# Two 1024-cubed projections of a transformer block as seven block products each, with their weight-side operands formed earlier

## The chip, the cores and the metric

The kernel runs on one core of a Trainium2 chip. It is hand-written for the engines: TensorE (PE) multiplies, VectorE (DVE), ScalarE (ACT) and GpSimd (POOL) do the elementwise work, and SyncE (SP) issues almost all transfers between HBM and the on-chip memory SBUF. The metric is the device time of one execution in microseconds (us); lower is better. Before the change it is 1440.81 us, the median of three executions (1439.41 to 1441.95).

## The reference

One layer of a mixer block on 1024 latent tokens and 256 context tokens of width 1024. A combined input projection feeds a convolution branch and an attention branch of 16 query heads on 4 key/value heads; two learned gates merge the branches, one output projection follows, and a normalised, gated residual ends the layer. Cut to what matters here:

```python
def merge_branches(y_conv, y_attn, gm, w_out):
    ga, gb = jnp.split(gm, 2, axis=-1)
    return (jax.nn.sigmoid(ga) * y_conv + jax.nn.sigmoid(gb) * y_attn) @ w_out
...
        o = latent_attention(q, k_all, v_all)
        y_attn = (o * jax.nn.silu(gate_b)) @ w_attn_out[l]
        y_conv = conv_module(ua, gate_a, conv_w[l], conv_b[l], ln_g[l], ln_b[l], w_conv_out[l])
        out = merge_branches(y_conv, y_attn, gm, w_out[l])
        x_new = x + gt[:, None, :] * rms_norm(out, g_post[l])
```

The change concerns the two products `@ w_attn_out` and `@ w_out`, each 1024 tokens by 1024 by 1024. `gt` is the third part of `silu(c) @ w_mod + b_mod`.

## The kernel before, in words

All products are carried out on float32 values that are split into a high part (a cast to the PE's reduced format) and a low part (the rest): `split` (L106) casts on ACT and subtracts on DVE or POOL, and `mm3` (L116) is one product of three matmuls, high by high, low by high and high by low. A "k step" below is one such group of three on 128 rows of the contraction and 512 columns. A 1024-cubed product has 8 x 2 output tiles of 128 x 512 and 8 k steps in each, that is 16 x 24 = 384 matmuls.

The program has stages. After the modulation and the normalisation comes the phase of **queries, keys and values** (L1171 to L1203): a loop over 4 key/value groups and 4 quarters of the tokens, 16 pieces in all. In each piece the PE computes one piece of q, k and v (24 x 2 matmuls into the PSUM tiles po, the values and keys and queries by tokens), transposes the one before, and works off `per` = 21 steps of `filler`. `filler(1)` takes one k step from a long stream of other projections (`proj`, L141: gates, convolution inputs), so that the PE always has something to do. `pump` interleaves the taps of the depthwise convolution on DVE. The attention stage (to L1305) interleaves score matmuls, softmax and value matmuls with the rest of the same stream, the last of which is the convolution's output projection. For each of 16 pairs (a head pair and a half of the tokens) `pair_end` (L862) divides the attention output O by its row sums, splits it in high and low and stores both to HBM (ogD).

The **tail** starts at L1309. `og_load` (L1038) reads the 32 halves of ogD (256 KB each) into `ogs` between the last filler steps. `attn_out_job` (L1046) is the attention projection: 8 output rows j x 2 halves hf x 24 matmuls; each output tile is gated and added to the convolution branch on DVE (from tgbD and mcD, the stored gate and gated convolution output), then split again for the next product. Beside it `wparts` loads and splits w_attn_out, and `wout_load` (L1072) loads and splits w_out. At (3, 1) of this loop `post_gate` (L1012) computes the vector gt: 8 loads of 512 KB of w_mod, two matmuls for each, a small round trip through HBM, and GP = the broadcast gate times the norm's weight. `w_out` (L1084) then runs over 8 rows of 128 tokens: 48 matmuls, ACT squares and sums, DVE scales, POOL takes the power for the norm, DVE adds the residual x, SP stores.

What sets the order: PE, DVE, ACT and POOL are wrapped (class `Ordered`, L41). While an engine is "held" it runs in the order of the program text; DVE, ACT and POOL are held up to the end of the q/k/v phase (L1215), the PE up to L1312. Where an engine isn't held, and on SP's queue everywhere, a scheduler places the instructions at build time. Every engine, SP too, runs its own list strictly in order: an instruction that waits stops all behind it. SP's transfers are assigned in turn to eight semaphores, and a transfer also waits for the one eight before it ("DMAHW0" to "DMAHW7" below). A tile name with n buffers (`tl(tag, shape, n)`) makes the n-th next tile of this name wait until the first has been read.

## Time and profile before

| | us |
|---|---|
| three executions, median (range) | 1440.81 (1439.41 to 1441.95) |
| the profiled execution, its own time | 1438.2 |
| its span in the trace (rows are counted from the span's start) | 1436.4 |
| PE busy | 1384.3 (96%) |
| DVE / ACT / POOL busy | 999.4 / 550.5 / 533.7 |
| first matmul of the attention projection | 1238.23 |
| first matmul of the output projection | 1342.85 |
| end of the last matmul | 1430.17 |

The profile gives, for one execution, the busy time of each engine (section 1), the span in 40 slices (section 2), the chain of work that ended last, followed back from the end (section 4), and groups of equal instructions (section 5). The chain is also printed in order of time: start, duration, engine and tile, and the number of instructions. Most lines carry L51, the line of the recording wrapper, so tiles and not lines tell the places apart: ppj, ps, pm and po are the PSUM tiles, ogs the loaded attention output, whi and wlo the split weights. A view of windows gives each engine's busy time in a stretch, with the DMA share and GB/s behind it.

### The profile page before, as it was taken

What the parts mean: (1) busy time and instruction counts of PE and PEld (TensorE: products, weight loads), DVE (VectorE), ACT (ScalarE), POOL (GpSimd) and SP (SyncE); (2) the same over time, 40 slices, a digit from 0 to 9 for tenths busy, and PEclk for the clock granted to TensorE, in tenths of its full rate; (3) what the DMA queues carried; (4) which work ended last, traced back from release to release, by engine and by line L of the source; (5) the groups of instructions that cost most, each with busy time, mean ns of one, the idle gap of its engine ahead of it and who ended that gap; (6) DMA issues with size and microseconds to landing.
All of it is one profiled execution on the core that took longest, in us unless ns stands there. A gap on an engine that the chain in (4) does not pass through costs nothing.

```text
span 1436.4 us, 18677 instructions
## 1 busy us (share of the span) xinstructions
PE 1384.3 (96%) x6584; PEld 1051.2 (73%) x6584; DVE 999.4 (70%) x1289; ACT 550.5 (38%) x1358; POOL 533.7 (37%) x359
## 2 busy tenths in 40 slices
PE   5988999999999999989999999999999999999998
PEld 3776889888888977756666766666766666676886
DVE  4478779888788898997688577777686643263532
ACT  5532334343443431334445454444543342031211
POOL 2124324233242220355577565666455553000000
PEclk9999999999999999999999999999999999999999
DMA  9513323224222329213355244644364223967522
GB/s 337 198 52 119 98 67 124 78 89 134 89 69 78 101 75 256 90 47 123 104 188 189 102 145 155 196 146 145 113 189 142 93 75 110 321 210 221 178 88 73
DMA packets 115898, 194.12 MB, mean 135 GB/s; under 512 B 16558, under 2 KB 46806, under 8 KB 115804
## 3 DMA queue, kind: packets, MB, share of 16 engines
q1 hardware_dynamic: 106076, 176.08, 37.6%
q10 hardware_dynamic: 9728, 16.85, 4.1%
q8 instruction: 52, 0.85, 0.2%
q14 instruction: 42, 0.34, 0.1%
HBM read 134.20 MB, written 58.55 MB: 134 GB/s over the span
## 4 chain that ended last, share of the span: by engine, by line
PE 78%; DVE 9%; DMA 5%; issue 3%; ACT 2%; POOL 2%; SPq 1%; ACTq 0%; DVEq 0%; POOLq 0%
PE ppj L51 33%; PE po L51 22%; PE ps L51 12%; PE pm L51 11%; DVE acc L51 3%; DMA ogs<-ogD 2%; DVE mx L51 1%; DVE y L51 1%; DMA wraw<-in_wch 1%; DVE ts L51 1%; DVE wlo L51 1%; DVE pconv L51 1%; DMA r<-r1D 1%; DMA wm<-in_wmod 1%; POOL wlo L51 0%
## 5 line engine op out<-in xcount | busy, mean ns | idle before, releaser
L51 PE MATMUL ppj<-t,whi 128*128 128x512 f32 x1728 | 611.9, 398 | 5.0 <-DVE t L51 2.6
L51 PEld LDWEIGHTS ppj<-t,whi 128*128 128x128 f32 x1728 | 326.5, 189 | 90.3 <-issue 17.7
L51 PE MATMUL ppj<-t,wlo 128*128 128x512 f32 x864 | 339.1, 392 | 3.1 <-POOL wlo L51 3.1
L51 DVE TENSOR_REDUCE mx<-pm 128x1 f32<-128x512 f32 (+1 forms) x320 | 213.5, 682 | 93.6 <-PE pm L51 91.0
L51 ACT ACTIVATE pe<-ps 128x512 f32<-128x512 f32 x320 | 190.2, 598 | 194.1 <-PE ps L51 166.4
L51 DVE SCALAR_TENSOR_TENSOR pconv<-y,cw,pconv 128x1020 f32<-128x1020 f32 (+14 forms) x157 | 200.8, 1279 | 7.4 <-ACT pconv L51 3.6
L51 POOL TENSOR_TENSOR psum<-psum,pe 128x512 f32<-128x512 f32 x128 | 190.2, 1503 | 36.6 <-ACT pe L51 32.5
L51 PE MATMUL ps<-r,kk 128*128 128x512 f32 (+1 forms) x640 | 200.8, 395 | 3.1 <-ACT pe L51 3.1
L51 PEld LDWEIGHTS ppj<-t,wlo 128*128 128x128 f32 x864 | 163.4, 189 | 33.0 <-POOL wlo L51 3.4
L51 PE MATMUL po<-pe,vt 128*64 128x512 f32 x640 | 144.4, 597 | 0.0
L51 PEld LDWEIGHTS ps<-r,kk 128*128 128x128 f32 (+1 forms) x640 | 119.6, 188 | 33.2 <-ACT pe L51 6.5
L51 PE MATMUL pm<-kk,r 128*128 128x512 f32 (+1 forms) x384 | 128.3, 363 | 8.3 <-DVE mx L51 8.0
L51 POOL TENSOR_TENSOR psum<-psum,part 128x512 f32<-128x512 f32 x64 | 88.1, 1379 | 124.7 <-DVE part L51 120.2
L51 PE MATMUL po<-wgh,t 128*128 128x384 f32 x512 | 133.4, 342 | 0.0
L51 POOL TENSOR_TENSOR wlo<-wraw,whi 128x512 fp32r<-128x512 f32 x57 | 79.9, 1414 | 119.4 <-ACT whi L51 96.1
L51 DVE SCALAR_TENSOR_TENSOR acc<-y,cw,acc 128x1017 f32<-128x1017 f32 (+14 forms) x77 | 114.5, 1499 | 0.7
L51 ACT CAST whi<-wraw 128x512 fp32r<-128x512 f32 x126 | 77.3, 630 | 76.0 <-PE ppj L51 45.0
L51 PEld LDWEIGHTS po<-pe,vt 128*64 128x64 f32 x640 | 43.1, 136 | 84.8 <-issue 84.8
L51 PEld LDWEIGHTS po<-wgh,t 128*128 128x128 f32 x512 | 95.6, 193 | 1.3
L51 PEld LDWEIGHTS pm<-kk,r 128*128 128x128 f32 x384 | 73.3, 191 | 27.5 <-DVE mx L51 10.8
L51 DVE TENSOR_TENSOR wlo<-wraw,whi 128x512 fp32r<-128x512 f32 x69 | 59.4, 862 | 46.0 <-ACT whi L51 39.9
L51 PE MATMUL po<-wgl,t 128*128 128x384 f32 x256 | 87.7, 342 | 3.0 <-POOL wgl L51 3.0
(209 smaller groups left out, 1581.5 us busy)
## 6 DMA issues: line engine op xcount, KB each, us to landing
wraw<-in_wch SPq DMA_DIRECT2D x96, 256.0 KB
wm<-in_wmod SPq DMA_DIRECT2D x16, 512.0 KB
r1D<-r1st SPq DMA_DIRECT2D x32, 256.0 KB
y<-accD SPq DMA_DIRECT2D x16, 512.0 KB
r<-r1D ACTq DMA_DIRECT2D x32, 256.0 KB
ogD<-og SPq DMA_DIRECT2D x32, 256.0 KB
ogs<-ogD SPq DMA_DIRECT2D x32, 256.0 KB
x<-in_x SPq DMA_DIRECT2D x8, 512.0 KB
```

The source lines that it names most:

```text
L51: i = f(*a, **k)
```

## The change

Both projections of the tail are computed as seven products of half-size blocks. Each operand is cut into 2 x 2 blocks of 512 x 512 (block number b = 2 x row half + column half); sums and differences of blocks (the tables LEFT, RIGHT and DATA) are multiplied in the order of `STEPS`, and the results are added up to the four output blocks. One of the 14 `block_step`s is 4 output tiles t x 4 k steps x 3 matmuls = 48 matmuls; 14 x 48 = 672 stand for 2 x 384 = 768.

The weight-side operands depend on weights alone. `operands()` makes them in the q/k/v phase: 16 batches (side 0 for w_attn_out, side 1 for w_out; 4 t; 2 halves u), each with 4 loads of 128 KB (`blk`, 4 buffers), then seven operands, of which four need a sum or difference on POOL; each operand is split (cast on ACT, difference on POOL, `opw`, 2 buffers) and stored to HBM (opD, 256 KB a time, 112 stores). The counter `rest` advances it: one operand per two filler steps, from the second piece on; `run(ops)` does what is left at the phase's end. The rope tables move to the same `blk` buffers.

The data-side operands are formed in the tail: `heads_load` reads the attention output (now stored once, unsplit, by `pair_end`) as 16 tiles O4; `data_split` forms sums on POOL in place and splits them. `coef_load` reads back a step's weight operands, 8 x 256 KB, two steps ahead, 28 MB in all. `merge` adds, gates and adds the convolution branch per output tile (its two inputs, 512 KB together, by `gate_ab`, three ahead); `finish` does norm and residual per output tile instead of per row of 128 tokens. `post_gate` runs earlier, spread between the last filler steps, with its loads two ahead. The PE stays held to the end.

```diff
+    SUB, ADD = ALU.subtract, ALU.add
+    LEFT = ((1, 0, None), (2, 1, None), (4, 3, None), (5, 3, (2, ADD, 3)), (7, 2, (0, SUB, 2)), (6, 0, (3, SUB, 0)),
+            (3, 1, (1, SUB, 0)))
+    RIGHT = ((1, 0, None), (2, 2, None), (3, 3, None), (5, 0, (1, SUB, 0)), (7, 1, (3, SUB, 1)), (6, 3, (3, SUB, 0)),
+             (4, 2, (2, SUB, 3)))
+    def operands():
+        for side in range(2):
+            for t in range(4):
+                for u in range(2):
+                    b = [tl("blk", (P, 256), 4, pool="A") for _ in range(4)]
+                    for i in range(4):
+                        r, c = divmod(i, 2)
+                        if side == 0:
+                            src = wao[t + 4 * r][:, 4 * c + 2 * u:4 * c + 2 * u + 2, :]
+                            SP.dma_start(out=b[i][:].rearrange("p (k c) -> p k c", c=P), in_=src)
+                        else:
+                            c0 = c * 512 + u * 256
+                            SP.dma_start(out=b[i][:], in_=wout[(t + 4 * r) * P:(t + 4 * r + 1) * P, c0:c0 + 256])
+                    yield 4
+                    for n, i, f in (LEFT, RIGHT)[side]:
+                        if f:
+                            G.tensor_tensor(out=b[i][:], in0=b[f[0]][:], in1=b[f[2]][:], op=f[1])
+                        w = tl("opw", (P, 2, 256), 2, F32R, "A")
+                        split(w[:, 0, :], w[:, 1, :], b[i][:], le=G)
+                        yield 2
+                        SP.dma_start(out=opD[side][n][t][:, :, u * 256:u * 256 + 256], in_=f32(w[:]))
...
         V.tensor_tensor(out=O[:], in0=O[:], in1=R[:], op=ALU.mult)
-        yield 2
-        hi, lo = tl("og", (P, 512), 2, F32R, "B"), tl("og", (P, 512), 2, F32R, "B")
-        split(hi[:], lo[:], O[:])
-        SP.dma_start(out=ogD[pr][0][:, tok], in_=f32(hi[:]))
-        SP.dma_start(out=ogD[pr][1][:, tok], in_=f32(lo[:]))
+        SP.dma_start(out=ogD[pr][:, tok], in_=O[:])
...
+        w = {}
+        def load(k):
+            w[k] = tl("y4", (P, T), 3)
+            SP.dma_start(out=w[k][:], in_=wmod[k * P:(k + 1) * P, 2 * D:3 * D])
+        for k in range(KD + 2):
+            if k < KD:
+                load(k)
+            if k > 1:
+                for hf in range(2):
+                    c = 64 * (k % 2) + 32 * hf
+                    PE.matmul(p[c:c + 2, :], sc[:, k - 2, :], w[k - 2][:, hf * 512:(hf + 1) * 512], start=(k < 4),
+                              stop=(k >= KD))
+            yield
...
+    STEPS = [(0, n) for n in (1, 5, 2, 7, 6, 3, 4)] + [(1, n) for n in (1, 7, 6, 5, 4, 3, 2)]
+    def heads_load():
+        O4.extend([[tl("O4", (P, 512), 16, pool="C") for _ in range(4)] for _ in range(4)])
+        for b in range(4):
+            if b == 3:
                 yield
...
+            r, c = divmod(b, 2)
+            for t in range(4):
+                SP.dma_start(out=O4[b][t][:], in_=ogD[t + 4 * r][:, c * 512:c * 512 + 512])
+    def coef_load(i):
+        side, n = STEPS[i]
+        coef[i] = []
+        for t in range(4):
+            src = opD[side][n][t]
+            if i % 2:
+                hi, lo = tl("whi", (P, 512), 4, F32R), tl("wlo", (P, 512), 4, F32R)
+            else:
+                hi, lo = tl("W", (P, 512), 8, F32R, "C"), tl("W", (P, 512), 8, F32R, "C")
+            for j, w in enumerate((hi, lo)):
+                SP.dma_start(out=f32(w[:]), in_=src[:, j, :])
+            coef[i].append((hi, lo))
+    DATA = [(0, None), (0, (1, SUB, 0)), (2, None), (1, (3, SUB, 1)), (0, (3, SUB, 0)), (3, None), (2, (2, SUB, 0)),
+            (0, None), (0, (0, SUB, 1)), (0, (3, SUB, 0)), (1, (1, ADD, 3)), (3, None), (0, (2, SUB, 0)), (2, None)]
+    def data_split(i):
+        blk = M4 if STEPS[i][0] else O4
+        b, f = DATA[i]
+        data[i] = []
+        for t in range(4):
+            if f:
+                G.tensor_tensor(out=blk[b][t][:], in0=blk[f[0]][t][:], in1=blk[f[2]][t][:], op=f[1])
+            hi, lo = tl("opd", (P, 512), 16, F32R, "C"), tl("opd", (P, 512), 16, F32R, "C")
+            split(hi[:], lo[:], blk[b][t][:])
+            data[i].append((hi, lo))
+    def gate_ab(n):
+        r, c = divmod(b, 2)
+        y = tl("y4", (P, 2, 512), 3)
+        SP.dma_start(out=y[:, 0, :], in_=tgbD[t + 4 * r][:, tok])
+        SP.dma_start(out=y[:, 1, :], in_=mcD[t + 4 * r][:, tok])
+        gates.append(y)
+    def merge(b, t, src, add):
+        m = M4[b][t] = tl("t2", (P, 512), 32)
+        y = gates.pop(0)
+        (G if b == 3 else V).tensor_tensor(out=m[:], in0=src, in1=add, op=ADD)
+        V.scalar_tensor_tensor(out=m[:], in0=y[:, 0, :], scalar=1.0, in1=m[:], op0=ADD, op1=ALU.mult)
+        V.scalar_tensor_tensor(out=m[:], in0=m[:], scalar=2.0, in1=y[:, 1, :], op0=ALU.mult, op1=ADD)
+        n = MERGE.index((b, t)) + 3
+        if n < len(MERGE):
+            gate_ab(n)
...
+    def finish(b, t, src, add, GP):
...
+        y = ys[m, c] = tl("t2", (P, 512), 32)
+        V.tensor_tensor(out=y[:], in0=src, in1=add, op=ADD)
+        junk = tl("junk", (P, 512), 1, pool="C")
+        S.activation(junk[:], y[:], AF.Square, accum_out=q[:, last:last + 1])
...
+            G.tensor_tensor(out=q[:, 3:4], in0=q[:, 2:3], in1=mhalf[:, 0:1], op=ALU.pow)
+        V.tensor_tensor(out=y[:], in0=y[:], in1=GP[:, d], op=ALU.mult)
+        if last:
+            for h in (1 - c, c):
+                y, d = ys[m, h], slice(h * 512, h * 512 + 512)
+                V.scalar_tensor_tensor(out=y[:], in0=y[:], scalar=q[:, 3:4], in1=xr[m][:, d], op0=ALU.mult, op1=ADD)
+                SP.dma_start(out=out[m * P:(m + 1) * P, d], in_=y[:])
+    def block_step(i, GP):
+        side, n = STEPS[i]
+        for t in range(4):
+            p = pt((XB, YB)[i % 2][t])
+            for k in range(4):
+                if side == 0:
+                    (whi, wlo), (mhi, mlo) = [[w[:, k * P:k * P + P] for w in coef[i][t]], [d[:] for d in data[i][k]]]
+                else:
+                    (whi, wlo), (mhi, mlo) = [[d[:, t * P:t * P + P] for d in data[i][k]], [w[:] for w in coef[i][k]]]
+                mm3(p[:], whi, wlo, mhi, mlo, k == 0, k == 3)
+            e = lambda j: tmp[side, j, t][:]
+            if n in (1, 5, 7):
+                g = tmp[side, n, t] = tl("O4", (P, 512), 16, pool="C") if side else tl("t2", (P, 512), 32)
+                S.copy(g[:], p[:])
+            if n == 6:
+                u = e(1)
+                if side:
+                    tmp[side, 0, t] = tl("O4", (P, 512), 16, pool="C")
+                    u = e(0)
+                V.tensor_tensor(out=u, in0=p[:], in1=e(1), op=ADD)
+                if side:
+                    G.tensor_tensor(out=e(7), in0=u, in1=e(7), op=ADD)
+                else:
+                    G.tensor_tensor(out=e(5), in0=u, in1=e(5), op=ADD)
+                    merge(3, t, e(5), e(7))
+                    G.tensor_tensor(out=e(7), in0=u, in1=e(7), op=ADD)
...
+                if g + q:
+                    if rest == 0:
+                        rest = next(ops, -1)
+                    rest -= 1
...
+    run(ops)
...
-    for _ in og_load():
-        filler(2)
+    heads = heads_load()
+    next(heads)
+    coef_load(0)
+    GP = tl("ysum", (P, T), 1)
+    for k, _ in enumerate(post_gate(GP)):
+        if k == 4:
+            run(heads)
+        filler(4)
+    data_split(0)
     run(fill)
-    PE.held = False
-    GP = tl("ysum", (P, T), 1)
-    run(stream([attn_out_job(j) for j in range(KD)], (KD - 2,)))
-    for m in range(NT):
-        w_out(m, GP)
+    coef_load(1)
+    data_split(1)
+    for n in range(3):
+        gate_ab(n)
+    for i in range(14):
+        block_step(i, GP)
+        if i + 2 < 14:
+            coef_load(i + 2)
+            data_split(i + 2)
```

Three places show what moves. First SP's queue where the old tail's loads stood, between the convolution projection's last stores (mcD). `ogs` is the loaded attention output; L1008 and L1043 are the stores and `og_load`. Before:

```order
L1043 DMA ogs_11202<-ogD_691 128x512 [waits DMAHW0_49,Pool_49]
L1043 DMA ogs_11203<-ogD_692 128x512 [waits DMAHW1_49,Pool_49]
L1043 DMA ogs_11204<-ogD_693 128x512 [waits DMAHW2_49]
...
L1043 DMA ogs_11210<-ogD_699 128x512 [waits DMAHW1_49]
L1043 DMA ogs_11211<-ogD_684 128x512 [waits DMAHW2_49]
L1008 DMA mcD_715<-ts_11412 128x512 [waits DMAHW3_49,DVE_49]
...
L1043 DMA ogs_11226<-ogD_699 128x512 [waits DMAHW2_49]
```

The program then begins the attention projection; the w_mod loads (`y<-in_wmod`) come 24 rows later, at row 613. In the changed kernel L1041 is the same store, L1052 the w_mod load of `post_gate`, L1090 the O4 loads and L1102 the operands' loads:

```order
L1052 DMA y_2928_11939<-in_wmod 128x1024 [waits PE_49]
...
L1090 DMA O_2896_11819<-ogD_688 128x512 [waits DMAHW0_49]
L1041 DMA mcD_707<-ts_11976 128x512 [waits DMAHW1_49,DVE_49]
L1090 DMA O_2897_11820<-ogD_689 128x512 [waits DMAHW2_49]
...
L1102 DMA W_11839<-opD_729 128x512 [waits DMAHW5_49]
...
L1102 DMA W_11852<-opD_732 128x512 [waits DMAHW4_49]
L1090 DMA O_2900_11823<-ogD_688 128x512 [waits DMAHW5_49]
...
L1090 DMA O_2903_11826<-ogD_691 128x512 [waits DMAHW0_49]
L1052 DMA y_2930_11960<-in_wmod 128x1024 [waits DMAHW1_49,PE_49]
L1052 DMA y_2932_11980<-in_wmod 128x1024 [waits DMAHW2_49,PE_49]
L1052 DMA y_2934_11997<-in_wmod 128x1024 [waits DMAHW3_49,PE_49]
```

The sixth w_mod load (y_2930) now stands behind fifteen loads of 256 KB, and these behind the store mcD_707, which waits for DVE.

Second, ACT in the q/k/v phase, at the second and third piece. Here `kst`/`r1st` are keys and queries after the transposes, `qk` the scaled queries and keys out of po, `vst` the values out of the next po. Before:

```order
L51 CAST r1st_1665<-pm_1659 64x2x256 [waits DVE_49]
L51 ACTIVATE ts_1641<-ppj_1642 128x512 [waits PE_49]
L51 ACTIVATE qk_1704<-po_1555,stat_1679 128x64 [waits Pool_49]
L51 ACTIVATE qk_1704<-po_1598,stat_1679 128x64 x5
L51 CAST whi_1726<-wraw_1696 128x512 [waits DMAHW4_49]
L51 CAST whi_1740<-wraw_1698 128x512 [waits DMAHW5_49]
L51 COPY vst_1763<-po_1765 128x64 [waits PE_49]
```

After:

```order
L51 CAST r1st_1729<-pm_1723 64x2x256 [waits DVE_49]
L51 CAST opw_1741<-blk_1697 128x256 [waits DMAHW5_49]
L51 CAST opw_1756<-blk_1698 128x256 [waits DMAHW7_49]
L51 ACTIVATE ts_1705<-ppj_1706 128x512 [waits PE_49]
L51 CAST opw_1768<-blk_1700 128x256 [waits DMAHW5_49,Pool_49]
...
L51 ACTIVATE qk_1779<-po_1654,stat_1746 128x64 x5
L51 CAST opw_1796<-blk_1700 128x256 [waits DMAHW6_49,Activation_49,Pool_49]
L51 CAST whi_1806<-wraw_1771 128x512 [waits DMAHW0_49]
L51 CAST opw_1812<-blk_1699 128x256 [waits DMAHW4_49,DMAHW7_49,Activation_49,Pool_49]
...
L51 CAST opw_1841<-blk_1698 128x256 [waits DMAHW2_49,Activation_49,Pool_49]
L51 COPY vst_1867<-po_1869 128x64 [waits PE_49]
```

Seven casts into opw, each of which waits for a blk load or a store of an earlier opw (DMAHW) or for POOL, stand ahead of and between the scaling of po and the copy of the next one.

Third, SP's queue near the end, where step 11 (n = 4) of the 14 ends: `t` and `y` are finished output tiles and residual rows, L1176 the stores of the result, L1150 the loads of x, whi/wlo the operands of the last step. Before, this stretch held only loads of x and stores (L1086, L1110):

```order
L1110 DMA out_x<-ts_12445 128x512 [waits DMAHW0_49,DVE_49]
L1086 DMA y_2952_12587<-in_x 128x1024 [waits DMAHW1_49]
L1110 DMA out_x<-ts_12482 128x512 [waits DMAHW2_49,DVE_49]
L1110 DMA out_x<-ts_12513 128x512 [waits DMAHW3_49,DVE_49]
L1086 DMA y_2960_12655<-in_x 128x1024 [waits DMAHW4_49]
L1110 DMA out_x<-ts_12550 128x512 [waits DMAHW5_49,DVE_49]
```

After:

```order
L1176 DMA out_x<-t_3228_13179 128x512 [waits DMAHW6_49,DVE_49]
L1176 DMA out_x<-t_3262_13304 128x512 [waits DMAHW7_49,DVE_49]
L1150 DMA y_3264_13315<-in_x 128x1024 [waits DMAHW0_49]
L1102 DMA whi_13395<-opD_765 128x512 [waits DMAHW1_49,PE_49]
...
L1102 DMA wlo_13396<-opD_765 128x512 [waits DMAHW5_49,PE_49]
...
L1176 DMA out_x<-t_3243_13248 128x512 [waits DMAHW1_49,DVE_49]
L1176 DMA out_x<-t_3274_13382 128x512 [waits DMAHW2_49,DVE_49]
L1150 DMA y_3276_13393<-in_x 128x1024 [waits DMAHW3_49]
L1102 DMA whi_13399<-opD_766 128x512 [waits DMAHW4_49,PE_49]
...
L1102 DMA wlo_13408<-opD_768 128x512 [waits DMAHW1_49,PE_49]
```

Loads of the last step's operands (opD_766 to opD_768) have moved behind eight stores of the result, which wait for DVE.

More of the change, by code (lines that the diff above doesn't have):

```diff
@@ L475, in block_kernel @@
     tgbD = [dram.tile([P, T], F32, name=nm("tgbD")) for _ in range(KD)]
-    ogD = [(dram.tile([P, T], F32, name=nm("ogD")), dram.tile([P, T], F32, name=nm("ogD"))) for _ in range(KD)]
+    ogD = [dram.tile([P, T], F32, name=nm("ogD")) for _ in range(KD)]
     gbD = [dram.tile([P, T], F32, name=nm("gbD")) for _ in range(KD)]
@@ L480, in block_kernel @@
     gtD = dram.tile([2, 512], F32, name="gtD")
+    opD = [[[dram.tile([P, 2, 512], F32, name=nm("opD")) for _ in range(4)] for _ in range(8)] for _ in range(2)]
     def kv_piece(src, vst, i):
@@ L1014, in post_gate @@
         p = pt("m")
-        for k in range(KD):
-            w = tl("y4", (P, T), 3)
-            SP.dma_start(out=w[:], in_=wmod[k * P:(k + 1) * P, 2 * D:3 * D])
-            for hf in range(2):
-                c = 64 * (k % 2) + 32 * hf
-                PE.matmul(p[c:c + 2, :], sc[:, k, :], w[:, hf * 512:(hf + 1) * 512], start=(k < 2), stop=(k >= KD - 2))
+        w = {}
[11 more added lines that the diff above has]
+            yield
         for hf in range(2):
@@ L1070, in block_kernel @@
-    wo = []
-    def wout_load(k):
-        if k < 3:
-            t = [tl("wo", (P, T), 4, F32R, "C") if k < 2 else tl("acc", (P, T), 2, F32R) for _ in range(2)]
-            parts = [[t[i][:, hf * 512:hf * 512 + 512] for hf in range(2)] for i in range(2)]
-        else:
-            parts = [[t[:] for t in i] for i in halves(1, "ogs", "C")[0]]
-        for hf in range(2):
-            raw = tl("ts", (P, 512), 4)
-            SP.dma_start(out=raw[:], in_=wout[k * P:(k + 1) * P, hf * 512:hf * 512 + 512])
-            split(parts[0][hf], parts[1][hf], raw[:])
-        wo.append(parts)
@@ new lines, in block_kernel @@
+    STEPS = [(0, n) for n in (1, 5, 2, 7, 6, 3, 4)] + [(1, n) for n in (1, 7, 6, 5, 4, 3, 2)]
+    XB, YB = ("s", "s", "pj", "pj"), ("m", "m", "o", "o")
+    O4 = []
+    M4 = [[None] * 4 for _ in range(4)]
+    data, coef, tmp, gates = {}, {}, {}, []
+    def heads_load():
+        O4.extend([[tl("O4", (P, 512), 16, pool="C") for _ in range(4)] for _ in range(4)])
+        for b in range(4):
+            if b == 3:
+                yield
+            r, c = divmod(b, 2)
+            for t in range(4):
+                SP.dma_start(out=O4[b][t][:], in_=ogD[t + 4 * r][:, c * 512:c * 512 + 512])
@@ new lines, in block_kernel @@
+    MERGE = [(b, t) for b in (0, 3, 1, 2) for t in range(4)]
+    def gate_ab(n):
+        b, t = MERGE[n]
+        r, c = divmod(b, 2)
+        y = tl("y4", (P, 2, 512), 3)
+        tok = slice(c * 512, c * 512 + 512)
+        SP.dma_start(out=y[:, 0, :], in_=tgbD[t + 4 * r][:, tok])
[10 more added lines that the diff above has]
+            gate_ab(n)
@@ new lines, in block_step @@
+    def block_step(i, GP):
[24 more added lines that the diff above has]
+                    G.tensor_tensor(out=e(7), in0=u, in1=e(7), op=ADD)
+            if side == 0:
+                if n in (2, 3, 4):
+                    merge({2: 0, 3: 1, 4: 2}[n], t, p[:], e({2: 1, 3: 5, 4: 7}[n]))
+            elif n == 5:
+                finish(3, t, p[:], e(7), GP)
+                G.tensor_tensor(out=e(0), in0=e(0), in1=e(5), op=ADD)
+            elif n in (2, 3, 4):
+                finish({2: 0, 3: 1, 4: 2}[n], t, p[:], e({2: 1, 3: 0, 4: 7}[n]), GP)
@@ L1171, in block_kernel @@
     per = (NF - done[0] - NB - 72) // 16
+    ops = operands()
+    rest = 0
     for g in range(NG):
```

82 lines of the change are left out of this document (24 added, 58 removed).

## The prediction

> **What bounds the kernel now.** I read the page's first part, then the chain, then the chain of the tail in order of time. The first two rows are from the page, the busy time of the engines and the chain's shares:
>
> ```profile
> PE 1384.3 (96%) x6584; PEld 1051.2 (73%) x6584; DVE 999.4 (70%) x1289; ACT 550.5 (38%) x1358; POOL 533.7 (37%) x359
> PE 78%; DVE 9%; DMA 5%; issue 3%; ACT 2%; POOL 2%; SPq 1%; ACTq 0%; DVEq 0%; POOLq 0%
> ```
>
> TensorE is busy for 1384.3 of 1436.4 us. So a matmul taken out is worth its time only where nothing else becomes late. The chain from 1224 us to the end (start, duration, what):
>
> ```profile
> 1210.29 11.80 PE ppj L51 x51
> ...
> 1224.57 2.98 DMA ogs<-ogD
> ...
> 1236.22 7.38 DMA ogs<-ogD
> ...
> 1248.75 5.34 DMA ogs<-ogD
> ...
> 1257.40 10.73 PE ps L51 x46
> 1268.13 10.88 PE pm L51 x48
> ...
> 1289.89 0.96 PE pm L51 x4
> ...
> 1342.85 11.15 PE ppj L51 x48
> ...
> 1419.28 10.89 PE po L51 x48
> ...
> 1430.25 0.60 ACT junk L51
> ...
> 1431.86 0.75 DVE ts L51
> ```
>
> In the tail 48 matmuls take 10.88 us, 0.2267 us each, and nearly nothing stands between them, but for the stretch up to 1257, where the loads of the attention output are in the chain. Its size comes from where the attention projection starts; two rows of PE's timeline:
>
> ```profile
> 1238.01 0.39 PE L51 MATMUL ppj<-t,whi 128*128 128x512 f32 x1
> 1238.23 0.39 PE L51 MATMUL ppj<-ogs,whi 128*128 128x512 f32 x1
> ```
>
> From 1238.23 to 1342.85 are 104.6 us. The work in it is 384 matmuls, 87.0 us, and the gate vector's 8 pieces of 0.96 us, 7.7. The rest, 9.9 us, is waiting for ogs and for split weights. After the last matmul (1430.17) come 6.2 us of norm, residual and store.
>
> **The change part by part.**
>
> *Matmuls.* 672 for 768: 96 x 0.2267 = **-21.8 us**. The waits of the old projection go with its loads: **-9.9**.
>
> *The start of the new tail.* The gate vector keeps its 7.7 us of matmuls, but between the last filler steps, and its loads pass through SP's queue. How fast these go is shown by SP's timeline and three windows (length, PE, PEld, DVE, ACT, POOL, granted clock, DMA share, GB/s):
>
> ```profile
> 1228.27 0.32 SPq L1008 DMA_DIRECT2D mcD<-ts  x1
> 1239.52 10.24 SPq L1043 DMA_DIRECT2D ogs<-ogD  x15
> 1225.00:1230.00 5.00, 5.00 (x24) 4.14 (x23) 0.69 (x1) 0.00 (x0) 0.00 (x0) 1.00 0.88 293
> 1240.00:1245.00 5.00, 4.76 (x19) 3.05 (x18) 0.79 (x2) 0.00 (x0) 0.00 (x0) 1.00 1.00 373
> 1260.00:1270.00 10.00, 10.00 (x45) 8.26 (x44) 6.84 (x12) 4.73 (x8) 0.00 (x0) 1.00 0.88 295
> ```
>
> 15 loads of 256 KB take 10.24 us, 0.683 each (373 GB/s). In the new order the sixth w_mod load stands behind 15 such loads, and these behind the store mcD_707, the store that is at 1228.27 now. Five gate pieces (4.8 us) now come ahead of it: SP passes it at about 1233. Then 15 x 0.683 = 10.2, 1.4 for the 512 KB themselves, and some 2 to 3 us until a load counts as landed (the first one above: 2.98). That is 1247 us. PE wants the load after 84 of its filler matmuls and the five pieces: 1210.3 + 19.0 + 4.8 = 1234 to 1235, so it stands still for **+12.0 us**; the filler is held to program order and can't slip past. If the scheduler's order meets earlier stores the wait shrinks; bounds 6 and 14. What is late next: the first block product, at 1258 for 1238.
>
> *Loads and elementwise work under the block products.* Each step of 10.88 us reads 2 MB of operands (190 GB/s), and in the steps that merge 2 MB of gates as well: 4.2 MB in 10.88 us is 385 GB/s, just over the 373 above. Two rows of DVE from the tail, where POOL is idle, and two from 600 to 1200 us, where it works, and POOL's price of a tile:
>
> ```profile
> L51 DVE TENSOR_TENSOR wlo<-wraw,whi 128x512 fp32r<-128x512 f32 x18 | 12.3, 690 | 22.2 <-ACT whi L51 22.0
> L51 DVE SCALAR_TENSOR_TENSOR ts<-ts,q,y 128x512 f32<-128x512 f32 x16 | 11.3, 749 | 0.9
> L51 DVE TENSOR_TENSOR wlo<-wraw,whi 128x512 fp32r<-128x512 f32 x40 | 39.5, 989 | 23.2 <-ACT whi L51 17.3 <-DMA y<-accD 5.9
> L51 DVE TENSOR_TENSOR O<-O,R 128x512 f32<-128x512 f32 x15 | 21.6, 1442 | 5.6 <-DMA R<-recD 5.6
> L51 POOL TENSOR_TENSOR wlo<-wraw,whi 128x512 fp32r<-128x512 f32 x44 | 57.5, 1317 | 76.8 <-ACT whi L51 53.5 <-issue 11.4 <-DMA vD<-vst 9.1
> ```
>
> Step 4 (n = 6) needs 12 additions on POOL, and the data of step 6 four more: 16 x 1.32 = 21 us beside 21.8 us of PE work in two steps. DVE needs 12 operations in a merging step (4 low parts, 4 x 2 or 3 for the merge): at 0.69 each 8 to 11 us, at the pace of PE. DVE's merges wait for POOL's sums, gate loads wait for the merges to free y4 (three buffers), and in SP's queue the last loads of step 7's operands stand behind these gate loads. I take **+5 us** of waiting there, from a lateness of 6 to 7 us of DVE (POOL's 21 us less the step and a half in which it may run), bounds 0 and 10. Near the end the last step's operands stand behind eight stores that wait for DVE's `finish` of step 11 (five operations of about 0.7 us for a tile): **+2.7**, bounds 0 and 5.
>
> *The end.* After the last tile come an addition, the square, the power, a scaling and two residuals, against a shorter list now: about two DVE tiles, 1.4, and a wait of DVE, 1.2, more: 8.8 for 6.2, **+2.6**.
>
> *Operands in the q/k/v phase.* PE is busy there without a gap (windows, and the chain of two pieces; then the waits of ACT and SP):
>
> ```profile
> 300.00:400.00 100.00, 100.00 (x499) 88.47 (x498) 83.43 (x100) 41.72 (x176) 34.63 (x23) 1.00 0.31 98
> 354.76 8.34 PE po L51 x48
> ...
> 378.13 8.34 PE po L51 x48
> ACT vst L51 <- PE po L51: 122.2, 29, 8.0
> SPq L592 <- ACT sq L51: 104.8, 15, 11.8
> ```
>
> A piece lasts 23.37 us. Prices of the added work, from these groups (150 to 640 us) and POOL's row above:
>
> ```profile
> L51 POOL TENSOR_TENSOR wgl<-wgr,wgh 128x768 fp32r<-128x768 f32 x12 | 22.1, 1851 | 36.6 <-ACT wgh L51 36.6
> L51 ACT CAST whi<-wraw 128x512 fp32r<-128x512 f32 x48 | 29.5, 648 | 8.2 <-PE ppj L51 6.1 <-DMA kk<-khiD 2.1
> L51 ACT CAST wgh<-wgr 128x768 fp32r<-128x768 f32 x12 | 9.7, 841 | 0.0
> ```
>
> 256 columns cost (1851 - 1317) = 534 ns on POOL, so a tile of 256 about 0.78 us, and on ACT 193 ns, so 0.45. Over the phase POOL gets 176 such, 137 us, 9.2 per piece (busy 35% then 74%); ACT gets 112, 50 us (42% then 56%); DMA gets 38 MB, some 108 GB/s on 98. All fit beside 23.37 us of PE as sums. As a chain they are tight: with two buffers in opw, operand n + 2 waits until operand n is stored. A store takes some 3 us from issue to landing, by these three small transfers of the chain:
>
> ```profile
> 1177.62 2.63 DMA dc<-og
> 1180.50 3.05 DMA recD<-rc
> 1184.21 3.02 DMA R<-recD
> ```
>
> Issue 0.3, landing 3.0, cast 0.45, difference 0.78, a sum 0.78 now and then: some 4.7 us for two, 2.35 for one; eight in a piece (7 operands, and a batch's loads of about 3 us) make 19 to 22 us of 23.37. ACT and POOL are in order, so a late store holds the next piece's copies out of po, and PE after 8 us of slack (the longest wait of ACT above). SP waits too, up to 11.8 us, for those copies. I put it at **+4 us**, nearest to the sums that fit; bounds 0 and 30, the upper one with each of 15 pieces 2 us longer.
>
> *Attention stage.* 16 casts, 16 differences and 16 stores fewer, all beside PE's matmuls: **-0.5**, bounds 0 and -2.
>
> Sum: -21.8 - 9.9 + 12.0 + 5 + 2.7 + 2.6 + 4 - 0.5 = -5.9. On the profiled execution, 1438.2 us (1436.4 of span and 1.8 around it), that gives 1432.3; the median of the runs lies 2.6 above that execution, so 1434.9; as the stall of 12 lies near the upper one of its bounds (6 and 14), I say **1434 us**.
>
> **The rivals.**
>
> *The operand chain stretches the pieces* (slower). Mechanism: opw's two buffers and SP's order hold ACT's copies out of po. It decides from about 9 us in the phase, where the gain is spent; for it speaks 19 to 22 of 23.37 us before any wait on SP, against it ACT's 8 us of slack. At 1 us more for each of 15 pieces the time is 1434 - 4 + 15 = 1445, at 2 us 1460; the middle, **1452**, is the price I give it.
>
> *The tail's waits are hidden* (much faster). Without the stall of 12 and the 7.7 in the steps: 1434 - 20 = 1414. For it speaks only that the SP order is the scheduler's and the loads ahead may be gone earlier; against it the queue's plain order.
>
> *Transfers bound the block products* (no change). The windows at 1225 and 1260 show 293 and 295 GB/s, where PE worked. 8.4 MB in two steps at 295 are 28.4 us against 21.8, twice in side 0: +13 for the 5, that is 1442.
>
> *DVE and POOL hold each other up* (no change). `O<-O,R` takes 1442 ns beside a busy POOL, a low part 690 without. If in steps 2 to 6 some 12 DVE operations with both inputs in SBUF take 0.75 more, DVE is 9 us later: 1443. For it speaks the pair of rows, against it the group at 989, a middle. [...]
>
> **How the numbers follow.** Forecast 0.40, operand chain 0.27, hidden waits 0.18, transfers 0.08, DVE with POOL 0.07. A measurement of this kernel can tell about 0.2% from no change, 2.9 us. The forecast's own range is 1428 to 1438, and with the hidden waits it makes faster 0.58; the two at 1442 and 1443 make no change 0.15; the chain makes slower 0.27. The range runs from 1418, which leaves half of the second case out, to 1452, which leaves half of the chain's out: 0.2 together.
>
> **What would show it.** Right: PE's pieces in the q/k/v phase at 23.4 to 23.7 us; one PE wait of about 12 us for a w_mod load near 1235; a wait of some us before step 7 and before the last step; 14 steps of 10.88 us; about 9 us after the last matmul. [...] The forecast falls if the phase's end moves by over 10 us or the tail has less than 10 us of waits.

## The result and the profile after

The change made the kernel slower: 1516.89 us (1515.84 to 1520.6, four executions) against 1441.22 us (1439.41 to 1441.95, four executions), a ratio of 1.0532 with a 95% interval of 1.0511 to 1.0553. The forecast was 1434 us with a range of 1418 to 1452. The page of the profiled execution, its engines and its chain:

```profile
PE 1384.9 (91%) x6488; PEld 1045.9 (69%) x6488; DVE 1041.2 (69%) x1317; ACT 596.3 (39%) x1486; POOL 739.4 (49%) x587
...
PE 50%; DVE 6%; DMA 3%; POOL 3%; issue 2%; ACT 2%; SPq 0%; ACTq 0%; POOLq 0%; DVEq 0%
```

PE has 96 matmuls fewer and is no less busy: the clock that it was granted was 0.968 on the mean, for 0.992 before, and the busy time per matmul rose from 210.3 to 213.5 ns. Its share of the span falls from 96% to 91% and its share of the chain from 78% to 50%. Two landmarks say where the time went: the first score matmul of the attention stage, and the last pair's row sums (`psum,ones`), with which the tail begins. In PE's timeline of the kernel before:

```profile
592.94 1.11 PE L51 MATMUL ps<-r,kk 128*128 128x512 f32 x4
...
1209.65 0.65 PE L51 MATMUL pm<-psum,ones 128*32 128x128 f32 x16
```

and of the changed kernel:

```profile
670.12 1.09 PE L51 MATMUL ps<-r,kk 128*128 128x512 f32 x4
...
1281.56 0.64 PE L51 MATMUL pm<-psum,ones 128*32 128x128 f32 x16
```

| stretch | before, us | after, us | difference | forecast |
|---|---|---|---|---|
| start to first score (has the q/k/v phase) | 592.9 | 670.1 | +77.2 | +4 |
| first score to last pair (attention) | 616.7 | 611.4 | -5.3 | -0.5 |
| last pair to end (tail) | 226.8 | 234.2 | +7.4 | -9.4 |

**The q/k/v phase.** Windows of the changed kernel (length, PE, PEld, DVE, ACT, POOL, granted clock, DMA share, GB/s); before, PE had 100.00 in the same row:

```profile
300.00:400.00 100.00, 83.52 (x397) 71.89 (x396) 66.10 (x76) 42.04 (x164) 60.83 (x62) 0.95 0.53 173
400.00:500.00 100.00, 87.89 (x415) 75.91 (x414) 74.69 (x85) 44.67 (x181) 61.94 (x63) 0.95 0.50 162
```

No engine is full, and PE waits for a seventh of the time. From the start of the first piece to that of the last a piece lasts 28.1 us on the mean, for 23.7 before. Who waits for whom, the longest totals from 160 to 600 us (total, times, longest):

```profile
ACT opw L51 <- POOL blk L51: 113.5, 47, 6.9
POOL opw L51 <- ACT opw L51: 100.6, 83, 13.2
DVE ts L51 <- ACT ts L51: 52.9, 13, 10.6
ACT opw L51 <- DMA opD<-opw: 40.7, 21, 5.2
```

ACT's casts of the operands wait for POOL's sums, POOL's differences for ACT's casts, and only the fourth row is the wait for opw's stores on which the prediction had put its price. How this gets to PE is seen in ten microseconds of the timeline (start, duration, what, and in brackets the idle time before it and what ended it):

```profile
245.33 1.30 POOL L51 TENSOR_TENSOR wlo<-wraw,whi 128x512 fp32r<-128x512 f32 x1
...
246.58 2.39 POOL L51 TENSOR_TENSOR ysum<-ysum,acc 128x1024 f32<-128x1024 f32 x1
...
248.91 0.74 POOL L51 TENSOR_TENSOR blk<-blk,blk 128x256 f32<-128x256 f32 x1
249.68 0.40 ACT L51 CAST opw<-blk 128x256 fp32r<-128x256 f32 x1 [6.92 <-POOL blk L51]
...
250.72 1.20 ACT L51 ACTIVATE pconv<-y,vec,cw 128x1024 f32<-128x1024 f32 x1
...
251.96 2.58 DVE L51 SCALAR_TENSOR_TENSOR pconv<-y,cw,pconv 128x1009 f32<-128x1009 f32 x2 [7.36 <-ACT pconv L51]
...
253.72 2.15 ACT L51 ACTIVATE qk<-po,stat 128x64 f32<-128x64 f32 x10
...
254.90 1.01 PE L51 MATMUL po<-wgh,t 128*128 128x384 f32 x2 [6.79 <-ACT qk L51]
```

In these rows POOL works without a pause, on older entries of its list. The sum (`blk`) that ACT wants comes after them; ACT stands 6.92 us in front of one cast of 0.40 us. Behind that cast stand, in ACT's order, the convolution's start, for which DVE stands 7.36 us, then a second cast with 1.49 us of the same waiting, and the scaling of po (`qk`), for which PE stands 6.79 us. Neither DVE's nor PE's work needs the result of the cast.

**The tail.** The chain of waits, at the three places that the prediction named (start, duration, what):

```profile
1314.73 5.95 DMA y<-in_wmod
...
1320.72 1.87 PE pm L51 x4
...
1419.38 3.81 DMA whi<-opD
...
1423.33 5.17 PE pm L51 x15
...
1487.58 5.69 DMA whi<-opD
...
1493.41 4.26 PE pm L51 x9
```

The waits of PE from 1281 to 1510 us:

```profile
PE pm L51 <- DMA y<-in_wmod: 12.7, 1, 12.7
PE pm L51 <- DMA whi<-opD: 11.6, 3, 4.4
PE pm L51 <- DMA wlo<-opD: 2.1, 1, 2.1
```

PE stands 12.7 us for the sixth w_mod load, 9.3 in three waits within the first tile of step 7, and 4.4 within that of step 13 (the second and third row hold these four: 11.6 + 2.1 = 9.3 + 4.4). After its last matmul, which ends at 1506.2, the span has 9.6 us more.

### The profile page after: what moved, and what is told of

It is laid out like the page before. It is cut to its first block, busy times and chain, and to the rows that moved or that the text cites. A ratio compares the mean times of both kernels' runs of the same rounds, so it can differ in the third digit from the quotient of the medians.

```text
span 1515.7 us, 19545 instructions
## 1 busy us (share of the span) xinstructions
PE 1384.9 (91%) x6488; PEld 1045.9 (69%) x6488; DVE 1041.2 (69%) x1317; ACT 596.3 (39%) x1486; POOL 739.4 (49%) x587
## 4 chain that ended last, share of the span: by engine, by line
PE 50%; DVE 6%; DMA 3%; POOL 3%; issue 2%; ACT 2%; SPq 0%; ACTq 0%; POOLq 0%; DVEq 0%
PE ppj L51 21%; PE po L51 11%; PE ps L51 11%; PE pm L51 8%; DVE t L51 1%; DVE acc L51 1%; DVE mx L51 1%; DMA whi<-opD 1%; POOL opw L51 1%; DMA r<-r1D 1%; DVE y L51 1%; POOL blk L51 1%; POOL q L51 0%; DMA W<-opD 0%; DMA y<-in_wmod 0%
## 5 line engine op out<-in xcount | busy, mean ns | idle before, releaser
L51 PE MATMUL ppj<-t,whi 128*128 128x512 f32 x1728 | 623.8, 403 | 28.4 <-DVE ts L51 13.4
L51 PEld LDWEIGHTS ppj<-t,whi 128*128 128x128 f32 x1728 | 330.6, 191 | 129.0 <-issue 24.3
L51 PE MATMUL ppj<-t,wlo 128*128 128x512 f32 x864 | 342.7, 397 | 3.1 <-POOL wlo L51 3.1
L51 DVE SCALAR_TENSOR_TENSOR pconv<-y,cw,pconv 128x1020 f32<-128x1020 f32 (+14 forms) x157 | 200.8, 1279 | 19.2 <-ACT pconv L51 15.4
L51 POOL TENSOR_TENSOR psum<-psum,pe 128x512 f32<-128x512 f32 x128 | 184.3, 1454 | 36.2 <-ACT pe L51 32.1
L51 POOL TENSOR_TENSOR opw<-blk,opw 128x256 fp32r<-128x256 f32 x112 | 84.8, 759 | 112.1 <-ACT opw L51 100.6
L51 ACT CAST opw<-blk 128x256 fp32r<-128x256 f32 x112 | 45.8, 415 | 168.3 <-POOL blk L51 113.5
L51 DVE SCALAR_TENSOR_TENSOR acc<-y,cw,acc 128x1019 f32<-128x1019 f32 (+14 forms) x77 | 111.2, 1458 | 0.6
L51 DVE SCALAR_TENSOR_TENSOR ts<-ts,ppj 128x512 f32<-128x512 f32 x46 | 31.6, 686 | 103.3 <-ACT ts L51 58.7
```

Source lines behind the costliest of these rows:

```text
L51: i = f(*a, **k)
```

## The experiments

The times stand beside a run of the kernel before on the same chip; one execution of each unless an interval is given. "Last pair" is the row of the landmark above (1209.65 before, 1281.56 changed).

**1. No operands (e_none).** The edit, with the operands' loads taken from another stored array of the same size:

```diff
-    ops = operands()
+    ops = iter(())
...
-                SP.dma_start(out=f32(w[:]), in_=src[:, j, :])
+                SP.dma_start(out=f32(w[:]), in_=gaD[(n + t) % 8][:, j * 512:j * 512 + 512])
```

> Leaves out the making of the operands in the q/k/v phase (no blk loads, sums, casts, differences or stores); the block products read the same number of bytes from another stored array instead, so the output is not the reference's. If the whole loss before the tail (first to last pair of the attention stage 72 us late) comes from this work, the last pair is back at 1210 us and the time is 1516.9 - 72 = 1445 us, with the tail as in the changed kernel (12.7 us for the w_mod load, some 10 before step 7, 4.6 before step 13). If something else of the change lengthens the phase or the attention stage (the rope tables' buffers, the unsplit attention output), it stays above 1460.

1444.65 us (before 1438.1). PE's timeline:

```profile
1208.91 0.64 PE L51 MATMUL pm<-psum,ones 128*32 128x128 f32 x16
```

The last pair is back where it was before the change. The whole loss ahead of the tail, 72 us, is the making of the operands; the rope tables' move to other buffers and the unsplit attention output cost nothing by themselves. The tail from here to the end is 234.0 us, as in the changed kernel: it is slower than before on its own account.

**2. Operands without their stores (e_nostore).** The line that stores opw to opD is left out; the tail loads from the other array, as in 1.

> Keeps the operands' loads, sums, casts and differences in the q/k/v phase but leaves out their 112 stores (block products read another stored array, output not the reference's). Theory A, opw's two buffers wait for the stores: the phase returns to within 10 us of the kernel without operands, 1445 to 1455 us. Theory B, ACT and POOL wait for each other in program order (ACT's cast for the POOL sum placed directly ahead, POOL's difference for that cast): at least half of the 72 us stays, 1480 to 1515 us. Theory C, the added transfers: as A.

1502.08 us (before 1438.1). Its waits from 160 to 590 us, and the landmark:

```profile
ACT opw L51 <- POOL blk L51: 135.4, 52, 6.9
POOL opw L51 <- ACT opw L51: 93.3, 73, 13.2
```

```profile
1265.89 0.65 PE L51 MATMUL pm<-psum,ones 128*32 128x128 f32 x16
```

Of 72.7 us (1281.56 - 1208.91) 57.0 stay. The stores, with opw's two buffers, account for the other 15.7: theory A is a fifth of the loss. Theory B, ACT and POOL waiting for each other in program order, fits the rest; that it is the order and not the amount of their work is shown only by 4 and 5.

**3. Loads and stores without the arithmetic (e_copyonly).** The blocks are stored as they were loaded (the four of a batch lie in one tile of one buffer, the rope tables in their own):

```diff
-                        if f:
-                            G.tensor_tensor(out=b[i][:], in0=b[f[0]][:], in1=b[f[2]][:], op=f[1])
-                        w = tl("opw", (P, 2, 256), 2, F32R, "A")
-                        split(w[:, 0, :], w[:, 1, :], b[i][:], le=G)
                         yield 2
-                        SP.dma_start(out=opD[side][n][t][:, :, u * 256:u * 256 + 256], in_=f32(w[:]))
+                        SP.dma_start(out=opD[side][n][t][:, :, u * 256:u * 256 + 256], in_=bb[:, i - i % 2:i - i % 2 + 2, :])
```

> Keeps the 64 loads and the 112 stores of 256 KB in the q/k/v phase but leaves out the operands' sums, casts and differences: the loaded blocks are stored as they are (output not the reference's). Theories A and B (waits of ACT and POOL): 1445 to 1455 us, as without operands. Theory C (the transfers and SP's queue themselves hold the phase up): over 1480 us.

1440.85 us (before 1438.1). A window of the phase:

```profile
200.00:500.00 300.00, 300.00 (x1505) 266.66 (x1504) 254.41 (x304) 125.78 (x525) 102.76 (x64) 1.00 0.58 190
```

PE is full again at twice the transfers. Theory C, the transfers, is out. And a phase that costs nothing does not make the change faster: the tail alone cancels what is saved.

**4. Operands in stages (e_lag).** Sum, cast, difference and store of one operand are no longer written one behind the other, but a slot apart. With it opw gets three buffers for two and blk eight for four, the loads come half a batch earlier, and the raw weights (wgr) have two buffers for four:

```diff
+        for m in range(7 * 16 + 3):
+            if m % 7 == 3 and m // 7 + 1 < 16:
+                load(*batches[m // 7 + 1])
...
+            if 0 <= m - 2 < 112:
+                b, side, t, u, n, i, f = todo[m - 2]
+                G.tensor_tensor(out=w[m - 2][:, 1, :], in0=b[i][:], in1=f32(w[m - 2][:, 0, :]), op=SUB)
+            if 0 <= m - 1 < 112:
+                b, side, t, u, n, i, f = todo[m - 1]
+                w[m - 1] = tl("opw", (P, 2, 256), 3, F32R, "A")
+                S.copy(w[m - 1][:, 0, :], b[i][:])
+            if m < 112:
+                b, side, t, u, n, i, f = todo[m]
+                if f:
+                    G.tensor_tensor(out=b[i][:], in0=b[f[0]][:], in1=b[f[2]][:], op=f[1])
+            yield 2 if m % 4 == 3 else 3
```

> The same operands in full, but in three stages a slot apart: the sum of operand m, the cast of m - 1, the difference of m - 2 and the store of m - 3 are written together, so that ACT finds its sum and POOL its cast finished; opw with 3 buffers, blk with 8, loads half a batch ahead, the raw weights of the q/k/v projections (wgr) with 2 buffers for 4. Theory B: most of the 72 us comes back, 1450 to 1475 us. Theory A with the stores the main cost: one buffer more gains little, 1490 us or more. POOL is then busy about three quarters of a piece.

1490.99 us (before 1438.1). The last pair moves from 1281.56 to 1252.57, by 29.0 us. Its waits from 160 to 600 us:

```profile
POOL stat L51 <- DVE stat L51: 76.0, 10, 15.2
ACT opw L51 <- DMA opD<-opw: 56.5, 39, 3.5
...
ACT opw L51 <- POOL blk L51: 41.6, 18, 5.9
```

The wait for POOL's sums falls from 113.5 to 41.6 us, and the wait for opw's stores does not fall (40.7, now 56.5), so the third buffer did not take that wait away; what each of these edits gave by itself was not told apart. The time is at the edge of what theory A had allowed and above B's 1475: B was too simple. POOL itself stands in its list, 76 us in all, at the power for the norms (`stat`), whose input comes from DVE's list.

**5. The power's input on POOL (e_lag2), 6. with other buffers (e_lag3).** In e_lag2 the store is written beside the difference, and

```diff
-        V.tensor_scalar(out=st[:], in0=st[:], scalar1=1.0 / HD, scalar2=EPS, op0=ALU.mult, op1=ALU.add)
+        G.tensor_scalar(out=st[:], in0=st[:], scalar1=1.0 / HD, scalar2=EPS, op0=ALU.mult, op1=ALU.add)
```

> The staged operands once more, with the store written in the same slot as the difference, and the small scaling ahead of POOL's power (stat) moved from DVE to POOL, so that POOL no longer waits for DVE's queue there (76 us of waiting in all, up to 15 at once). If these waits of POOL in program order pass on to ACT and PE, 1455 to 1475 us for 1491; if the pieces are now long because ACT, POOL and DVE are full as sums, 1485 to 1495.

1470.84 us (before 1441.29), last pair at 1233.77. POOL, ACT and DVE do the same sums, casts and differences as in the changed kernel, and 47.8 of the 72.7 us are gone. Most pieces now last 23.4 to 24.8 us; three stay at 28 to 30, the first pieces of the second, third and fourth group. I took the raw weights' buffers for the cause, which the staged kernels had cut from four to two:

```diff
-            raws.append(tl("wgr", (P, 2, 384), 2, pool="wg"))
+            raws.append(tl("wgr", (P, 2, 384), 4, pool="wg"))
...
-        hi, lo = tl("kst", (HD, 256), 8, F32R, pool), tl("kst", (HD, 256), 8, F32R, pool)
+        nk = 2 if pool == "A" else 8
+        hi, lo = tl("kst", (HD, 256), nk, F32R, pool), tl("kst", (HD, 256), nk, F32R, pool)
```

> The staged operands with POOL's own scaling, but the raw weights of the q/k/v projections (wgr) back at 4 buffers; the room for blk and opw comes from the keys' staging tiles (kst, 2 buffers for 8). In the kernel with 2 buffers the pieces that stay long, 28 to 30 us, are those in which a new group's weights are split (ACT waits up to 3.5 us for a wgr load). If that is the cause, all pieces are 23.3 to 24.5 us and the time is 1445 to 1455 us; if POOL's and ACT's sums bind in these pieces, they stay at 27 us or more and the time at 1465 or more.

1472.33 us (before 1439.84), last pair at 1234.38: no change, a miss. What POOL does ahead of the second of the long pieces (it begins at 339.9 us), while the next group's weights are split:

```profile
328.21 1.30 POOL L51 TENSOR_TENSOR wlo<-wraw,whi 128x512 fp32r<-128x512 f32 x1
329.46 0.75 POOL L51 TENSOR_TENSOR opw<-blk,opw 128x256 fp32r<-128x256 f32 x1
330.16 0.74 POOL L51 TENSOR_TENSOR blk<-blk,blk 128x256 f32<-128x256 f32 x1
330.85 1.85 POOL L51 TENSOR_TENSOR wgl<-wgr,wgh 128x768 fp32r<-128x768 f32 x1
...
333.08 1.96 POOL L51 TENSOR_TENSOR stat<-stat,mhalf 128x10 f32<-128x10 f32 x1
335.01 1.85 POOL L51 TENSOR_TENSOR wgl<-wgr,wgh 128x768 fp32r<-128x768 f32 x1
```

In these rows it is busy with gaps of 0.1 us at most: the differences of 1.85 us for the next group's weights come on top of all else, ACT and DVE fall behind, and in the next piece PE waits for DVE's rotary operations (18.3 us of waiting in the phase). The share of POOL over the phase, two thirds, had hidden that it is full at such places.

**7. The tail's waits (e_tail, e_lag2_tail).** e_tail changes the tail alone: the gate vector moves into step 8, the merge's gates get five buffers, the last step's operands other buffers and an earlier load.

```diff
+        if i == 7:
+            vec_gate = post_gate(GP)
...
+        block_step(i, GP, vec_gate if i == 8 else None)
...
+        y = tl("y4", (P, 2, 512), 3) if n % 5 < 3 else tl("acc", (P, 2, 512), 2)
```

> The changed kernel with the tail's three waits taken out: the gate vector's matmuls move from the filler into block step 8, after the merges (their w_mod loads no longer behind the loads of O4 and the first operands); the merge's gates get five buffers for three; the last step's operands go into other buffers and are loaded from step 9 on. Theory of the prediction (these waits are SP's order): the stretch from the last pair to the end falls from 233.8 us by 13 + 10.5 + 4.6 of waiting and a few us of half clock, to 200 to 210, and the time to 1485 to 1495. Rival, the transfers themselves or POOL and DVE bound the block products: the waits before the first and the last step go but 8 us or more stay before step 7, and new ones come in step 8: 220 or more.

1511.35 us (before 1441.29); the tail is 230.5 us (1509.6 - 1279.1) for 234.2. The wait for w_mod went from 12.7 to 8.9 us only, now inside step 8; step 13's wait is gone, step 7 has 4.5 us left, and the end after the last matmul grew to 13. Of the rival's reading the new waits in step 8 and the 220 us or more came, the 8 us before step 7 did not. e_lag2_tail has both edits, 5 and 7:

> Both edits, the staged operands with POOL's own scaling and the tail without its three waits. As the two lie in different stretches their gains should add: the time of the staged kernel alone less some 25 to 30 us, 1430 to 1450; if the tail's gain depends on the phase, less.

1466.37 us (before 1441.29); the tail is 227.9 us. The tail is 7.3 us shorter than with edit 5 alone (235.2), the time 4.5, and not 25 to 30.

**8. The gate vector first (e_best), no operands in the full pieces (e_best2).** e_best has the phase of e_lag3 and the buffers of e_tail. In it the w_mod loads come ahead of all others, the odd steps' operands go through ACT's queue, and half of the final scalings through POOL:

```diff
-    next(heads)
-    coef_load(0)
     GP = tl("ysum", (P, T), 1)
     for k, _ in enumerate(post_gate(GP)):
-        if k == 4:
-            run(heads)
-        filler(4)
+        filler(2)
+        if k == 5:
+            next(heads)
+        if k == 7:
+            coef_load(0)
+    run(heads)
```

> The same phase with another tail: the gate vector in the first half of the filler with its w_mod loads ahead of the loads of O4 and of the first operands; five buffers for the merge's gates; the odd steps' operands loaded through ACT's queue, those of the last step early into other buffers; in finish, the scaling of a row's first half on POOL. If the tail's waits are the order of SP's queue, no wait of over 3 us stays in the block products and the stretch from the last pair to the end is 205 to 212 us for 233.8: with the phase at 1445 to 1455 the time is 1418 to 1432 us, below the kernel before the change. If transfers or DVE bind the block products, 1435 or more.

1465.42 us, ratio 1.0186 (1.0156 to 1.0217). The wait for w_mod is gone (0.4 us), but the tail is still 225.6 us where 205 to 212 were expected. PE's waits from 1235 to 1450 us:

```profile
PE pm L51 <- DVE opd L51: 5.0, 3, 4.0
PE pm L51 <- DMA whi<-opD: 4.8, 1, 4.8
PE ps L51 <- DVE opd L51: 1.9, 2, 1.3
```

Where SP's order no longer holds PE up, DVE does (`opd`, the split data), and the first operands. e_best2 adds the skip in the phase (the other pieces take an operand every two slots for every three), step 1's operands through ACT's queue, and the addition and square of `finish` ahead of older work:

```diff
-                if g + q:
+                if g + q and (q < 3 or g == NG - 1):
...
+        with urgent():
+            V.tensor_tensor(out=y[:], in0=src, in1=add, op=ADD)
+            S.activation(junk[:], y[:], AF.Square, accum_out=q[:, last:last + 1])
```

> Staged operands as before, but none in the three pieces in which the next group's weights are split on POOL and ACT (the other pieces take one operand per two slots for one per three), and the other tail with the first odd step's operands also through ACT's queue and finish's addition and square ahead of the older tiles' remaining operations. If POOL's sum binds in the long pieces (four differences of 1.85 us, 7 to 8 operands, wlo, the power: about 25 us against 23.4), all pieces fall to 23.3 to 24.5 us, the first score matmul comes at 595 to 602 us for 620 and the time is 1435 to 1445 us, with 8 us or less after the last matmul. If the long pieces have another cause, four of them stay at 28 us and the time at 1455 or more.

1451.64 us, ratio 1.0085 (1.0058 to 1.0113). Timeline:

```profile
607.89 1.47 PE L51 MATMUL ps<-r,kk 128*128 128x512 f32 x4
...
1224.39 0.65 PE L51 MATMUL pm<-psum,ones 128*32 128x128 f32 x16
```

The long pieces are gone, which bears out that POOL was full there: from the start of the first piece to that of the last it takes 362.1 us, for 355.1 before the change. The first score still comes 15 us late: with the phase over, the rotary operations of the last piece are late on DVE and hold PE for 8 us. Of what was expected, the pieces came; the time (1435 to 1445) and the end (8 us; it is 12) did not.

**9. A phase for nothing, and the best tail (e_copy_tail).** The operands of experiment 3 (blocks stored as loaded) with the tail of e_best2.

> The operands' loads and stores without their sums, casts and differences (blocks stored as loaded, output not the reference's), together with the last of the other tails: what the block products would be worth if the operands cost the q/k/v phase nothing. The phase took nothing from that (last pair at 1206 to 1210 us), and this tail took 224 us with the operands made in full: 1431 to 1436 us, faster than before by 0.3 to 0.6%, a quarter of the 21.8 us of matmuls saved. If DVE's lateness from the phase is what the tail still pays, 1420 to 1428; if the tail is bound by its own transfers and by DVE, 1430 or more.

1438.39 us (1434.43 to 1440.77) against 1438.59 (1434.81 to 1442.63), ratio 0.9995 (0.998 to 1.001): no difference. The tail, 1207.91 to 1438.4, is 230.5 us; the same tail took 224.7 in e_best2. Why it is longer here was not found; the profiled execution, 1440.17 us, is one of the slowest of the ten. Its windows, the whole of the tail's products and two of its tight places:

```profile
1208.00:1426.00 218.00, 201.75 (x843) 153.95 (x843) 132.08 (x167) 57.72 (x113) 98.19 (x65) 0.96 0.74 247
1250.00:1300.00 50.00, 43.54 (x169) 34.57 (x170) 23.07 (x26) 12.13 (x21) 18.44 (x12) 0.90 0.96 324
1337.00:1365.00 28.00, 21.38 (x73) 14.89 (x72) 24.38 (x25) 6.02 (x11) 19.42 (x12) 0.88 0.83 290
```

against the same stretch of the kernel before:

```profile
1210.00:1430.00 220.00, 216.84 (x935) 166.40 (x927) 84.22 (x140) 42.44 (x84) 3.87 (x7) 1.00 0.55 183
```

Here is the answer to what the block products are worth in this tail: PE's work falls, DVE's rises from 84 to 132 us, POOL's from 4 to 98, the transfers from 183 to 247 GB/s, and PE waits in turn for loads (share 0.96 at 1250 to 1300) and for DVE (24.4 of 28 us at 1337 to 1365). 21.8 us of matmuls are saved and as much is spent: PE's waits come to 16.4 us (8.3 for loads of W, 5.6 for DVE's split data, 1.4 and 1.1 for w_mod and ACT), the rest is mostly a lower clock behind the waits (0.96 for 1.00) and 12 us of end for 6.

## Why the prediction was wrong

**The step that failed** is "Operands in the q/k/v phase", priced at +4 us with bounds of 0 and 30; it measured +77 to the first score, of which 5 came back in the attention stage. That the operands hold ACT's work on po was the first rival, at 0.27. It named the place, but the cause that it gave, opw's two buffers and SP's order, is a fifth of the loss, and its price, 1 to 2 us for each of 15 pieces, was too low by a factor of 2.5 to 5. Three things went wrong in the sum:

- The durations were right: 759 ns forecast as 0.78 us for POOL's difference, 757 for its sum, 415 as 0.45 us for ACT's cast. What was wrong was to add them up as one chain of 2.35 us per operand. Each link of it stands in a list that runs in order, behind whatever else is in that list: a sum waited behind 1.30 and 2.39 us of POOL's other work in the rows above, and ACT then 6.92 us behind the sum. POOL's shares of before, 34 of 100 us, I took as free time at any moment.
- "PE after 8 us of slack" was taken once for a piece. The slack is real, but one wait of 6.9 us in front of one cast uses most of it up, and a piece holds seven or eight such casts.
- The part that I priced, opw's two buffers and the store's landing, was 15.7 of 72.7 us (experiment 2).

**The tail's terms** held in kind and mostly in size. Matmuls: 10.88 us in a step without waits, as before. The stall for the sixth w_mod load: +12.0 forecast, 12.7 measured; SP passed the store ahead of the loads at 1233.0 us (1304.90, less the 71.9 us by which the tail begins later) for 1233 forecast. Step 7: +5 forecast with bounds 0 and 10, 9.3 measured, by the path that was named: DVE's merges, then the gates' loads, then the operands' loads. The lateness of DVE behind that +5 was itself mis-summed: 21 us less a step and a half (16.3) are 5, not 6 to 7. Last step: +2.7, measured 4.4. End: 8.8, measured 9.6. The tail is 16.8 us off, of which these four explain 7.5. Another 7.8 are the half clock behind the waits (0.50 granted, below), for which the sum had no term: 1.6 us behind the w_mod load, 3.5 in step 7 (23.7 us for 10.88, of which 9.3 are waits) and 2.7 in step 13 (18.0 us, of which 4.4).

**The attention stage** gave 5.3 us for 0.5 forecast, but none where the phase is on time or 15 us late (616.9 us in e_none, 616.5 in e_best2, 616.7 before the change). What came back is thus part of the phase's own lateness, and the 16 splits fewer are worth nothing.

**The other rivals.** "Hidden waits" (1414) fell: the order of SP's queue held. "Transfers bound the block products" (1442) has its share in experiment 9. "DVE and POOL hold each other up": in the phase DVE's rotary operations with two inputs in SBUF took longer beside a busier POOL (61 of 100 us, for 34). In the changed kernel, 160 to 600 us (before: 383, 556 and 824 ns):

```profile
L51 DVE TENSOR_TENSOR qkt<-qk,rope 128x64 f32<-128x64 f32 (+1 forms) x62 | 25.8, 457 | 1.0 <-ACT qk L51 1.0
L51 DVE TENSOR_TENSOR qk<-qk,rope 128x128 f32<-128x128 f32 (+1 forms) x30 | 21.5, 717 | 1.0
L51 DVE TENSOR_TENSOR qk<-qk,qkt 128x640 f32<-128x640 f32 x15 | 14.0, 934 | 0.5
```

The taps (`pconv`, 157 in both kernels), whose running sum lies in PSUM, stayed at 1279 ns; why the one took longer and not the other was not shown. By these rows (4 x 74 + 2 x 161 + 110 ns) it costs some 0.7 us per piece, not the time lost.

**What stays open.** How far the remaining 15 us before the first score in e_best2 are DVE's lateness from the phase, and how far the operands left over at its end, was not told apart, nor which of DVE and the loads would bind the tail next.

## What to carry to other kernels

Where engines run their lists in order, work added "beside" a full engine must be priced by the list it is put into: for each new instruction, what may stand ahead of it in its own list and in its producer's, at the place where both are busiest, not by the mean share over the phase. Write the links of such work a slot apart, so that none waits; that, with earlier loads and the power's input moved off DVE, took 48 of 72 us away here. And a scheme that trades matmuls for additions and transfers pays only where the helpers have room in that very stretch: here the tail's DVE and POOL work rose by 48 and 94 us to save 21.8 us of PE.
